# Hybrid attention block: the first eight row blocks of attention groups 1 to 7 are taken in the order 4, 0, 5, 1, 6, 2, 7, 3

## The chip, the cores and the metric

The kernel runs on one core of a Trainium2 chip. The metric is the device time of one execution in microseconds. Before the change it is 2704.64 us, the median of three runs (2703.09 to 2706.77).

The core's engines each work through a list of instructions of their own, in order: TensorE (PE in the profile) multiplies matrices, VectorE (DVE), ScalarE (ACT) and GpSimd (POOL) do the elementwise work, and SyncE (SP) issues DMA transfers. They wait for each other through semaphores.

## What is computed

One layer of a transformer block over 2048 rows of width 1024: normalise, project, two kinds of attention side by side, an output projection, and a gated feed-forward layer (the FFN). Cut to what the change touches:

```python
proj = einsum('bsd,de->bse', rms_norm(h, norm1_w), w_in)
dq, dk, dv, sq, sk, sv = split(proj, SPLIT_POINTS, axis=-1)
# 4 heads of differential attention: two softmax maps per head
p = softmax(dq . dk * scale + bias[t5_bucket(k_pos - q_pos)], masked by chunks of 64)
y_diff = (p[0] - lam * p[1]) @ dv, normalised per head
# 8 heads of stick-breaking attention
z = sq . sk * scale                       # strictly causal: key < query
log_1mb = log_sigmoid(-z)
a = exp(log_sigmoid(z) + reversed exclusive cumsum of log_1mb over the keys)
y_sb = a @ sv, normalised per head
h = h + concat(y_diff, y_sb) @ w_out
h = h + SwiGLU(rms_norm(h, norm2_w))
```

Every query row is independent of every other, so the order in which blocks of rows are taken changes nothing in the result.

## The kernel before

The 2048 rows are 16 row blocks of 128. The attention is done in eight groups, one after the other: groups 0 to 3 are one head of differential attention each (the softmax groups, `diff_attn`), groups 4 to 7 two heads of stick-breaking attention each (`sb_attn`). Both are causal, so row block i needs the keys of blocks 0 to i: its work grows with i, and rows 0 to 3 together have 10 of a group's 136 blocks of scores. ("Row 4" is short for row block 4 below.)

**Projection.** Before a group's attention can read its queries, keys and values, they are projected tile by tile (a tile is one row block; 24 matmuls on line 325, or 72 short ones on line 341 in groups 4 to 6, which are "turned": they come out transposed). In the other groups the tiles are gathered in batches of four: `raw` holds the projected queries and keys, `proj_batch` (lines 386 to 414) squares, sums, takes a root (`rs`, a power on POOL), scales, splits each number into two halves of 16 bits (`st`), and turns the batch with DMA transposes (line 409) into `qT` and `kT`. Group 7 has only the split and the transposes. Batch 1, tiles 4 to 7, has to be there before row 4's scores can be made.

**Softmax row** (`probs`, lines 521 to 569): scores in PSUM (`sc`, line 506); VectorE copies them out with the running maximum (line 542, and line 546 where the bias applies); ScalarE takes the exponential with its sum (line 556); VectorE combines the two maps (lines 561 to 566); `split_t` (lines 449 to 461) splits the result into two halves (`s16`; casts on ScalarE or POOL, the subtraction on POOL, line 98) and turns it with a DMA transpose into `aT`; then the values are multiplied in (`pv`, line 517) two row blocks later.

**Stick-breaking row** (`stage_a`, lines 602 to 627): scores; two sigmoids on ScalarE (lines 618 and 619); a running product over the keys on VectorE (line 621); a product (line 622); `split_t`; and `pv` some seven pieces later (`pend`).

**Accumulators.** The values of four row blocks (two in group 7) share one PSUM accumulator `yp`. After the last of them `finish` (lines 464 to 496) squares, sums, scales, turns on TensorE (line 488), writes two halves `mo` (lines 492 and 493) and stores. There are two `yp` buffers, taken in turn; a buffer is free again when `mo` is written. `aT` has six buffers.

**Order.** The Python loops emit instructions with a priority; a scheduler that runs when the kernel is built then lays out each engine's list. Scores and the row's elementwise work have a higher priority (`"at": 200`), projections a lower one (`"pm": -200`), so projections are put where TensorE would have nothing better. `advance` (line 778) emits the projection tiles, eight ahead at a group's end: when group g starts, tiles 0 to 7 of it have been emitted. The main loop is at lines 862 to 868; the output projection's row blocks are mixed into group 7, then the FFN follows.

Of the kernel before, what the change touches and what calls it, by code (L numbers as in the profile page):

```python
# [11 lines left out]
F32 = mybir.dt.float32  # L12
# [47 lines left out]
def block(tc, a, out):  # L60
# [3 lines left out]
    with top:  # L64
# [44 lines left out]
        def nm(s):  # L109
            uid[0] += 1  # L110
            return f"{s}{uid[0]}"
# [144 lines left out]
        with ExitStack() as ph1:  # L256
# [207 lines left out]
            def finish(g, G, i, k, yp, ssum=None):  # L464
# [30 lines left out]
                note("D", 350 * k + 200)  # L495
                SP.dma_start(ms[i - k + 1 : i + 1, :, g, :].rearrange("i p n -> p i n"), mo[:, :k].rearrange("p i s n -> p i (s n)"))

            def fq(g, i):
                k = 2 if g == NG - 1 else 4
                return (i % k, k)  # L500
# [18 lines left out]
            def diff_attn(g, G):  # L519
                @pri("at")  # L520
                def probs(i):
                    L = (i + 1) * 128
                    near = max(0, i - 1) * 128
                    nb = i // 8 + 1
                    zs = [[], []]
                    if i % 4 == 0:
                        sums[0] = sm.tile([P, 4, 2], F32, tag="sums", bufs=3, name=nm("sums"))
                    su = sums[0][:, i % 4, :]
                    mx = sm.tile([P, 2, 8], F32, tag="mx", name=nm("mx"))
                    for m in range(2):  # L530
                        nx = 0
                        for b in range(nb):
                            n = min(1024, L - 1024 * b)
                            z = z4()
                            for c in range((n + 511) // 512):
                                lo, hi = 512 * c, min(512 * c + 512, n)
                                sc = ps.tile([P, 512], F32, tag="sc", bufs=4, name=nm("sc"))
                                score_chunk(G, sc, i, 2 * b + c, m, (hi - lo) // P)
                                f = min(max(near - 1024 * b - lo, 0), hi - lo)
                                note("D", 1.05 * (hi - lo) + 200)  # L540
                                if f > 0:
                                    DVE.tensor_scalar(z[:, lo : lo + f], sc[:, :f], kz_d[:], None, op0=ALU.mult, op1=ALU.max, accum_out=mx[:, m, nx : nx + 1])
                                    nx += 1
                                if f < hi - lo:
                                    b0 = 1024 * b + lo + f - (i - 1) * 128
                                    DVE.tensor_tensor_reduce(z[:, lo + f : hi], sc[:, f : hi - lo], bias[:, g, b0 : b0 + hi - lo - f], kz_d[:], -3.0e38, ALU.add, ALU.max, mx[:, m, nx : nx + 1])
                                    nx += 1
                            zs[m].append((b, n, z))
                    ng = sm.tile([P, 2], F32, tag="ng", name=nm("ng"))
                    if nx > 1:  # L550
                        DVE.tensor_reduce(ng[:], mx[:, :, :nx], op=ALU.max, axis=AX.X)
                    ACT.activation(ng[:], ng[:] if nx > 1 else mx[:, :, 0], AF.Identity, bias=lnc[:], scale=-1.0)
                    s2 = sm.tile([P, 2, 2], F32, tag="s2", name=nm("s2")) if nb > 1 else None
                    for m in range(2):
                        for b, n, z in zs[m]:
                            ACT.activation(z[:, :n], z[:, :n], AF.Exp, bias=ng[:, m : m + 1], accum_out=(s2[:, m, b : b + 1] if nb > 1 else su[:, m : m + 1]))
                            note("A", 0.84 * n + 300)
                    if nb > 1:
# [3 lines left out]
                    DVE.tensor_scalar(rc[:], rc[:], mlam[:], su[:, 0:1], op0=ALU.mult, op1=ALU.mult)  # L562
                    note("D", 600)
                    aTs = []
                    for (b, n, z0), (_, _, z1) in zip(*zs):
                        DVE.scalar_tensor_tensor(z0[:, :n], z1[:, :n], rc[:], z0[:, :n], op0=ALU.mult, op1=ALU.add)
                        note("D", 1.05 * n + 130)
                        aTs.append((b, n, split_t(z0[:, :n], n)))
                    return aTs

                sums = {}
                ypd = {}

                def values(i, aTs, ssum):
                    r, k = fq(g, i)
                    if r == 0:
                        ypd[0] = ps.tile([P, 512], F32, tag="yp", name=nm("yp"))
                    yp = ypd[0]
                    for q, (b, n, aT) in enumerate(aTs):
                        pv(G, yp, P * r, aT, b, n, 0, 128, r == 0 and q == 0, r == k - 1 and q == len(aTs) - 1)  # L580
                    if r == k - 1:
                        finish(g, G, i, k, yp, ssum)

                held = []
                for i in range(NT):
                    if i % 4 == 0:
                        level()
                    held.append((i, probs(i), sums[0]))
                    if len(held) > 2:
                        values(*held.pop(0))  # L590
                    yield ((i + 1) * (i + 2) / 2 + CD * (i + 1)) / (136 + 16 * CD), i + 1
                for u in held:
                    values(*u)

            def sb_attn(g, G):
# [39 lines left out]
                def stage_c(i, m, b, n, aT):  # L635
                    r, k = fq(g, i)
                    if i // k not in ypd:
                        ypd[i // k] = ps.tile([P, 512], F32, tag="yp", name=nm("yp"))
                    yp = ypd[i // k]
                    pv(G, yp, P * r + 64 * m, aT, b, n, 128 * m, 64, r == 0 and m == 0 and b == i // 8, r == k - 1 and m == 1 and b == 0)  # L640
                    if m == 1 and b == 0 and r == k - 1:
                        finish(g, G, i, k, yp)
                        G["fin"] = i + 1

                pend = []
                done = 0
                for i in range(NT):
                    if i % 4 == 0:
                        level()
                    for b in range(i // 8, -1, -1):  # L650
                        for m in range(2):
# [5 lines left out]
                            yield done / (272 + 48 * CS), (i + 1 if b == 0 and m == 1 else i)  # L657
                for u in pend:
                    stage_b(*u)

# [199 lines left out]
            outs = 0  # L860
            advance(NT - LAG0)
            for g in range(NG):
                advance(NT * g + 4)
                for fr, i in (diff_attn if g < 4 else sb_attn)(g, Gs[g]):
                    advance(max(NT * g + min(4 * (i // 4 + 1), NT), int(NT * (g + 1 + fr) - (LAG * (1 - LF * fr * (g == NG - 1)) if g else LAG0 + (LAG - LAG0) * fr))))
                    while g == NG - 1 and len(wos) == 4 and outs < Gs[g].get("fin", 0) and (outs + 2) * (outs + 3) / 272 < fr - LO:
# [431 lines left out]
```

## Time and profile before

| | |
|---|---|
| median of three runs | 2704.64 us |
| profiled execution: its time | 2702.93 us |
| its span in the profile | 2701.0 us (1.93 us lie around it) |
| first projections and group 0, to its last score | 0 to 203 us |
| groups 1 to 3 (softmax), to the last score of group 3 | 203 to 602 us |
| groups 4 to 6 (stick-breaking), to the last score of group 6 | 602 to 1086 us |
| group 7 with most of the output projection | 1086 to 1351 us |
| the rest of the output projection and the FFN | 1351 to 2701 us |

A group is counted here from the last score of the group before it, since the engines run on across the border. The FFN is nearly all matmuls. The change touches the starts of groups 1 to 7, from the last score of row 15 to the first score of row 8 of the next group: 406.6 us in sum.

How to read the rows: the table of stretches gives, for each stretch, its length, then each engine's busy time and number of instructions, the granted TensorE clock (1.00 is full), the share of the DMA engines' time and the rate. A group of instructions gives line, engine, operation, tiles, shapes and count, then busy time, the mean ns of one, and the idle time before them with what ended it. A row of the timeline gives start and length in us, and in brackets the idle time before it and what ended it. Matmuls overlap, so that the mean of one is longer than the time from one to the next; busy time over count is nearer to that.

### The profile page before, as it was taken

What the parts mean: (1) busy time and instruction counts of PE and PEld (TensorE: products, weight loads), DVE (VectorE), ACT (ScalarE), POOL (GpSimd) and SP (SyncE); (2) the same over time, 40 slices, a digit from 0 to 9 for tenths busy, and PEclk for the clock granted to TensorE, in tenths of its full rate; (3) what the DMA queues carried; (4) which work ended last, traced back from release to release, by engine and by line L of the source; (5) the groups of instructions that cost most, each with busy time, mean ns of one, the idle gap of its engine ahead of it and who ended that gap; (6) DMA issues with size and microseconds to landing.
All of it is one profiled execution on the core that took longest, in us unless ns stands there. A gap on an engine that the chain in (4) does not pass through costs nothing. (4 is left out here: it accounts for less than half of the span.)

```text
span 2701.0 us, 50505 instructions
## 1 busy us (share of the span) xinstructions
PE 2508.6 (93%) x19628; PEld 1507.6 (56%) x19628; DVE 1959.8 (73%) x3712; ACT 1344.7 (50%) x2487; POOL 1517.8 (56%) x1097
## 2 busy tenths in 40 slices
PE   7998989899988989889999999999999999999999
PEld 4655656577776776567774444444444444444444
DVE  6898879899989889887866877778685543433434
ACT  4665656567978878765634534435352112111121
POOL 2578767768767767545665755665564332322323
PEclk9999999999999999999999999999999999999999
DMA  6778697768989989997996566565748744635532
GB/s 221 211 163 184 143 200 172 172 145 183 195 175 185 178 166 206 208 205 203 230 317 232 211 232 219 207 239 183 253 171 330 304 159 157 234 132 184 202 110 94
DMA packets 619584, 534.40 MB, mean 198 GB/s; under 512 B 480640, under 2 KB 548224, under 8 KB 609104
## 3 DMA queue, kind: packets, MB, share of 16 engines
q1 hardware_dynamic: 617520, 529.09, 70.1%
q8 instruction: 154, 2.52, 0.4%
q0 software_dynamic: 512, 1.36, 0.2%
q14 instruction: 86, 0.70, 0.1%
q10 hardware_dynamic: 1312, 0.72, 0.1%
HBM read 261.08 MB, written 147.32 MB: 151 GB/s over the span
## 5 line engine op out<-in xcount | busy, mean ns | idle before, releaser
L98 POOL TENSOR_TENSOR s<-z,s 128x1024 f16<-128x1024 f32 (+7 forms) x288 | 471.5, 1646 | 141.8 <-ACT s L89 118.2
L506 PE MATMUL sc<-kT,qT 128*128 128x512 f16 (+3 forms) x1520 | 382.7, 354 | 51.1 <-DVE z L622 18.6
L1104 PE MATMUL pd<-wd,act 128*128 128x512 f16 x1764 | 392.8, 380 | 5.3 <-DVE cu L1038 4.7
L621 DVE TENSOR_TENSOR_SCAN z<-z,sc 128x512 f32<-128x512 f32 (+3 forms) x320 | 352.8, 1112 | 56.5 <-ACT sc L619 34.6
L325 PE MATMUL pj<-w,xt 128*128 128x384 f16 x1920 | 354.6, 333 | 17.1 <-ACT raw L374 5.8
L1004 PEld LDWEIGHTS <-wu 128*128 128x128 f16 x1848 | 181.9, 98 | 224.6 <-issue 12.8
L1004 PEld LDWEIGHTS <-wg 128*128 128x128 f16 x1848 | 181.3, 98 | 222.9 <-issue 9.3
L517 PE MATMUL yp<-v,aT 128*128 128x64 f16 (+1 forms) x4896 | 271.2, 205 | 36.9 <-DMA aT<-s 35.7
L517 PEld LDWEIGHTS <-aT 128*128 128x128 f16 x4896 | 239.1, 100 | 114.4 <-DMA aT<-s 46.7
L98 POOL TENSOR_TENSOR act<-cg,act 128x512 f16<-128x512 f32 x109 | 150.7, 1393 | 259.4 <-ACT act L1063 259.4
L1104 PEld LDWEIGHTS <-act 128*128 128x128 f16 x1764 | 172.9, 98 | 213.5 <-issue 7.2
L325 PEld LDWEIGHTS <-xt 128*128 128x128 f16 x1920 | 187.8, 99 | 147.2 <-issue 23.4
L89 ACT CAST s<-z 128x128 f16<-128x128 f32 (+7 forms) x215 | 173.3, 810 | 135.9 <-DMA aT<-s 44.6
L98 POOL TENSOR_TENSOR stages<-stages 128x512 f32<-128x512 f32 x97 | 171.4, 1767 | 116.5 <-DVE wg L220 42.2
L618 ACT ACTIVATE z<-sc,c 128x512 f32<-128x512 f32 (+3 forms) x320 | 211.2, 665 | 24.4 <-PE sc L506 12.4
L98 POOL TENSOR_TENSOR hs<-hs,cu 128x512 f32<-128x512 f32 x102 | 133.6, 1317 | 159.3 <-DVE hs L1110 59.7
L506 PEld LDWEIGHTS <-qT 128*128 128x128 f16 x1520 | 128.8, 99 | 119.7 <-issue 23.9
L831 PE MATMUL po<-wo,mt 128*128 128x256 f16 x1536 | 182.4, 279 | 12.6 <-DVE xf L834 8.6
L1063 ACT CAST act<-cg 128x512 f16<-128x512 f32 x126 | 76.7, 616 | 231.1 <-DVE cg L1069 192.7
L1110 DVE SCALAR_TENSOR_TENSOR hs<-pd,c,hs 128x512 f32<-128x512 f32 x144 | 106.0, 747 | 115.0 <-PE pd L1104 105.3
L341 PE MATMUL pj<-xt,w 128*128 128x128 f16 x2304 | 177.4, 222 | 6.2 <-DVE v L363 5.2
L1004 PE MATMUL pm<-X,wu 128*128 128x512 f16 x792 | 179.8, 381 | 2.1 <-ACT cg L1049 1.7
(254 smaller groups left out, 4812.3 us busy)
## 6 DMA issues: line engine op xcount, KB each, us to landing
xt<-xs SPq DMA_DIRECT2D x112, 512.0 KB, 4.5
hs<-hd SPq DMA_DIRECT2D x72, 512.0 KB, 4.5
hd<-hs SPq DMA_DIRECT2D x56, 512.0 KB, 5.9
split<-wg SPq DMA_DIRECT2D x11, 1792.0 KB, 6.9
split<-wu SPq DMA_DIRECT2D x11, 1792.0 KB, 6.7
split<-wd SPq DMA_DIRECT2D x11, 1792.0 KB, 6.8
wg<-split SPq DMA_DIRECT2D x11, 1792.0 KB, 7.5
wd<-split SPq DMA_DIRECT2D x11, 1792.0 KB, 9.0
```

The lines of the kernel that those rows point to most:

```text
L89: ACT.copy(dst, src)
L98: (DVE if e == "D" else POOL).tensor_tensor(dst, a_, b_, op)
L325: PE.matmul(pj[:, :384], lhsT=xv[:, xi, kt, :], rhs=G["w"][:, wi, kt, :], start=n == 0, stop=n == 23)
L341: PE.matmul(o, lhsT=x_ if c == 2 else w_, rhs=w_ if c == 2 else x_, start=n == 0, stop=n == 23)
L506: last = PE.matmul(sc[:, : 128 * w].rearrange("p (t n) -> p t n", n=P), lhsT=G["q"][i // 4][:, a_, i % 4, :], rhs=G["k"][q][:, b_, 0:w, :] ...
L517: PE.matmul(yp[:, y0 : y0 + wd], lhsT=aT[:, a_, :], rhs=v[:, v_ : v_ + wd], start=start and j == 0 and q == 0, stop=stop and j == nb - 1 a ...
L618: ACT.activation(om[:, lo:hi], sc[:, :w], AF.Sigmoid, scale=G["nkz"][:])
L621: DVE.tensor_tensor_scan(ov, ov, sc[:, :w], om[:, hi : hi + 1], op0=ALU.mult, op1=ALU.bypass)
L831: PE.matmul(po[:, sl], lhsT=mt[:, kt, P * xi : P * xi + P], rhs=wos[2 * h + n][wi][:, kt, :], start=q == 0, stop=q == 23)
L1004: PE.matmul(ps_[:].rearrange("p (t n) -> p t n", n=P), lhsT=wv[:, wo, wi, 128 * kt : 128 * kt + 128], rhs=X[xo][:, :, xi, kt, :], start=st ...
L1104: PE.matmul(po[:], lhsT=act[:, ao, xi, 128 * j : 128 * j + 128], rhs=W["d"][:, wo, wi, :], start=start and u == 0 and q == 0, stop=u == nu ...
L1110: DVE.scalar_tensor_tensor(dst, po[:], kd[:], src, op0=ALU.mult, op1=ALU.add)
```

## The change

Groups 1 to 7 take their first eight row blocks in the order 4, 0, 5, 1, 6, 2, 7, 3, and then 8 to 15 as before. Group 0 keeps the old order. What depended on rows coming in turn is now kept by number: the sums and the accumulator belong to i // 4, so two accumulators are open at once; the count of finished rows is kept as a set; the progress that paces the projections is summed over the rows taken; and group g starts only after eight of its tiles have been emitted, not four.

```diff
+            def row_order(g):
+                pairs = [i for j in range(4) for i in (4 + j, j)]
+                return (pairs if g > 0 else list(range(8))) + list(range(8, NT))
...
-                        sums[0] = sm.tile([P, 4, 2], F32, tag="sums", bufs=3, name=nm("sums"))
-                    su = sums[0][:, i % 4, :]
+                        sums[i // 4] = sm.tile([P, 4, 2], F32, tag="sums", bufs=3, name=nm("sums"))
+                    su = sums[i // 4][:, i % 4, :]
...
-                        ypd[0] = ps.tile([P, 512], F32, tag="yp", name=nm("yp"))
-                    yp = ypd[0]
+                        ypd[i // 4] = ps.tile([P, 512], F32, tag="yp", name=nm("yp"))
+                    yp = ypd[i // 4]
...
-                for i in range(NT):
-                    if i % 4 == 0:
+                order = row_order(g)
+                done = 0
+                for at, i in enumerate(order):
+                    if at % 4 == 0:
                         level()
-                    held.append((i, probs(i), sums[0]))
+                    held.append((i, probs(i), sums[i // 4]))
                     if len(held) > 2:
                         values(*held.pop(0))
-                    yield ((i + 1) * (i + 2) / 2 + CD * (i + 1)) / (136 + 16 * CD), i + 1
+                    done += i + 1 + CD
+                    yield done / (136 + 16 * CD), max(order[: at + 2])
...
-                        G["fin"] = i + 1
+                        ended.update(range(i - k + 1, i + 1))
+                        G["fin"] = next(t for t in range(NT + 1) if t not in ended)
...
-                advance(NT * g + 4)
+                advance(NT * g + 4 * (row_order(g)[0] // 4 + 1))
```

What the scheduler makes of it is seen in the engines' lists. First, ScalarE where group 5 starts. L618 and L619 (L625 and L626 in the change) are the two sigmoids, with the width of the chunk at the end; a row of 512 columns with number 11454 is the last of group 4's row 15; L89 is a cast of `split_t`, L349 the copy-out of a projected pair of tiles, L475 and L153 belong to `finish`. Before:

```order
L619 ACTIVATE sc_11454<-sc_11454,c_6511 128x512
L618 ACTIVATE z_11752<-sc_11754,c_8728 128x128
L619 ACTIVATE sc_11754<-sc_11754,c_8727 128x128
L89 COPY s_11414<-z_11395 128x1024
L618 ACTIVATE z_11769<-sc_11771,c_8728 128x128
L619 ACTIVATE sc_11771<-sc_11771,c_8727 128x128
L349 ACTIVATE qT_10979<-pj_10981,half_79 128x256
L618 ACTIVATE z_11786<-sc_11788,c_8728 128x256
```

and with the change:

```order
L626 ACTIVATE sc_11454<-sc_11454,c_6508 128x512
L89 COPY s_11414<-z_11395 128x1024
L349 ACTIVATE qT_10214<-pj_10578,half_79 128x256
L89 COPY s_11462<-z_11443 128x1024
L349 ACTIVATE qT_10979<-pj_10981,half_79 128x256 x2
L475 ACTIVATE y_11735<-yp_10871 128x512
L153 ACTIVATE yrs_11739<-yss_11736,c_6507 128x8
L625 ACTIVATE z_11752<-sc_11763,c_8718 128x512
L626 ACTIVATE sc_11763<-sc_11763,c_8717 128x512
L625 ACTIVATE z_11752<-sc_11754,c_8718 128x128
```

The sigmoids of rows 0 and 1 (128 and 256 wide) stood right behind row 15; now casts, copies and a `finish` stand there, and the next sigmoids are row 4's (512 + 128 wide).

Second, POOL where group 2 starts. `rs839`, `raw808` and `st807` are batch 1 of group 2 (the power, the product with the gain and the two subtractions); L93 and L98 on `s16` are the casts and subtractions of `split_t` for a row, 128 to 384 wide for rows 0 to 2; L219 splits the next group's weights. Before:

```order
L156 TENSOR_TENSOR rs839_4403<-rs839_4403,mh1_77 128x16
L93 TENSOR_SCALAR s16853_4550<-z4847_4532 128x128
L93 TENSOR_SCALAR s16862_4574<-z4856_4556 128x256
L219 TENSOR_SCALAR w16889_4680<-wst888_4676,sW893_4684 128x1536 x2
L93 TENSOR_SCALAR s16871_4601<-z4865_4580 128x384
L98 TENSOR_TENSOR s16853_4550<-z4847_4532,s16853_4550 128x128
L98 TENSOR_TENSOR s16862_4574<-z4856_4556,s16862_4574 128x256
L98 TENSOR_TENSOR raw808_4174<-raw808_4174,gk_222 128x4x128
L98 TENSOR_TENSOR st807_4173<-raw808_4174,st807_4173 128x4x2x64
```

and with the change:

```order
L219 TENSOR_SCALAR w16885_4677<-wst884_4673,sW889_4681 128x1536 x2
L98 TENSOR_TENSOR s16802_4125<-z4788_4077,s16802_4125 128x896
L156 TENSOR_TENSOR rs839_4403<-rs839_4403,mh1_77 128x16
L93 TENSOR_SCALAR s16828_4285<-z4813_4234 128x1024
L98 TENSOR_TENSOR s16830_4291<-z4816_4243,s16830_4291 128x1024
L98 TENSOR_TENSOR s16828_4285<-z4813_4234,s16828_4285 128x1024
L98 TENSOR_TENSOR raw808_4174<-raw808_4174,gk_222 128x4x128
L98 TENSOR_TENSOR st807_4173<-raw808_4174,st807_4173 128x4x2x64 x2
```

Five instructions of rows 0 to 2 and two of the weights stood between the power and the gain of batch 1; now three of group 1's row 15 do, and the weights come earlier.

Third, TensorE in group 2, where `finish` turns the accumulator of rows 4 to 7 and row 8's values are multiplied in. L488 is the turn of `finish` (`yp942` is rows 4 to 7 before, `yp906` rows 0 to 3 with the change, where the turn of rows 4 to 7, `yp878`, stands 17 rows further up); `yp1029` is the accumulator of rows 8 to 11, `aT978` and `aT973` row 8. Before:

```order
L517 LDWEIGHTS aT978_5080
L517 MATMUL yp1029_5325<-v806_4172,aT978_5080 128x128
L488 MATMUL yp942_4885<-id32_63,y1004_5219 128x128 x4
L517 LDWEIGHTS aT978_5080
L517 MATMUL yp1029_5325<-v806_4172,aT978_5080 128x128
```

and with the change:

```order
L488 MATMUL yp906_4730<-id32_63,y1004_5219 128x128 x4
L510 LDWEIGHTS qT1034_5413
L510 MATMUL sc1086_5678<-kT781_4050,qT1034_5413 128x512
L510 LDWEIGHTS qT1034_5413
L510 MATMUL sc1086_5678<-kT781_4050,qT1034_5413 128x512
L510 LDWEIGHTS qT1034_5413
L510 MATMUL sc1087_5682<-kT837_4399,qT1034_5413 128x512
L510 LDWEIGHTS qT1034_5413
L510 MATMUL sc1087_5682<-kT837_4399,qT1034_5413 128x512
L521 LDWEIGHTS aT973_5068
L521 MATMUL yp1029_5325<-v724_3713,aT973_5068 128x128
```

Row 8's values ran while rows 4 to 7 were being finished; now they stand behind the turns of both accumulators.

More of the change, by code (lines that the diff above doesn't have):

```diff
@@ L642, in stage_c @@
                         finish(g, G, i, k, yp)
-                        G["fin"] = i + 1
+                        ended.update(range(i - k + 1, i + 1))
+                        G["fin"] = next(t for t in range(NT + 1) if t not in ended)
                 pend = []
                 done = 0
-                for i in range(NT):
-                    if i % 4 == 0:
+                ended = set()
+                order = row_order(g)
+                for at, i in enumerate(order):
+                    if at % 4 == 0:
                         level()
@@ L656, in sb_attn @@
                             done += n // P + CS
-                            yield done / (272 + 48 * CS), (i + 1 if b == 0 and m == 1 else i)
+                            yield done / (272 + 48 * CS), (max(order[: at + 2]) if b == 0 and m == 1 else max(order[: at + 1]))
                 for u in pend:
```

## The prediction, made before the changed kernel had run

> **What bounds the kernel now.** I read the page's first and fourth parts, then the table of stretches around each group's start, then groups of instructions by line and form, and last the timeline at two places.
>
> ```profile
> PE 2508.6 (93%) x19628; PEld 1507.6 (56%) x19628; DVE 1959.8 (73%) x3712; ACT 1344.7 (50%) x2487; POOL 1517.8 (56%) x1097
> 1443.25 2.76 PE pd L1004 x12
> ```
>
> The second row is where the chain of waits begins: followed back from the end it stays in the FFN and says nothing of the attention. The change touches only the attention, so the question is when that ends, and this has to be read from stretches. First the seven starts, each from the last score of row 15 to the first score of row 4 of the next group, and their sum:
>
> ```profile
> 203.40:223.90 20.50, 17.48 (x173) 12.34 (x171) 19.48 (x62) 15.09 (x39) 17.54 (x10) 0.99 0.65 152
> 336.70:378.70 42.00, 35.83 (x296) 24.59 (x295) 27.03 (x79) 21.59 (x62) 31.45 (x23) 0.92 0.84 171
> 469.30:513.50 44.20, 36.87 (x309) 24.43 (x306) 36.08 (x85) 23.82 (x67) 34.78 (x22) 0.92 0.69 167
> 602.40:624.30 21.90, 19.80 (x291) 18.17 (x289) 19.24 (x47) 17.51 (x36) 15.30 (x12) 0.92 0.82 202
> 760.80:777.80 17.00, 14.83 (x269) 13.05 (x266) 13.86 (x30) 11.19 (x25) 12.29 (x10) 0.90 1.14 219
> 918.20:936.40 18.20, 13.94 (x285) 12.17 (x282) 16.02 (x34) 11.07 (x24) 11.75 (x9) 1.00 0.93 188
> 1086.10:1120.90 34.80, 30.24 (x326) 20.04 (x325) 30.58 (x62) 20.59 (x43) 24.23 (x18) 1.00 0.90 198
> sum 198.60, PE 168.99 PEld 124.79 DVE 162.29 ACT 120.86 POOL 147.33; mean PE 24.14 PEld 17.83 DVE 23.18 ACT 17.27 POOL 21.05
> ```
>
> Then the sum of the seven stretches from row 4's first score to row 8's, with group 1's as one row of them, and the sum of the stretches from there to the group's last score (for group 7, to 1351 us):
>
> ```profile
> 223.90:254.90 31.00, 27.27 (x185) 15.97 (x186) 28.89 (x79) 15.49 (x44) 22.95 (x18) 0.90 0.84 197
> sum 208.00, PE 178.50 PEld 126.89 DVE 175.24 ACT 148.32 POOL 125.26; mean PE 25.50 PEld 18.13 DVE 25.03 ACT 21.19 POOL 17.89
> sum 741.00, PE 681.59 PEld 516.55 DVE 651.77 ACT 536.56 POOL 515.99; mean PE 97.37 PEld 73.79 DVE 93.11 ACT 76.65 POOL 73.71
> ```
>
> TensorE is busy 85% of the starts, 86% of rows 4 to 7 and 92% of the rest; VectorE 82%, 84% and 88%. No engine bounds the first 407 us: TensorE idles 29.6 us in the starts and 29.5 us in rows 4 to 7. This is the most that a better order could take directly from those stretches. After row 8 TensorE is nearer to being the bound than VectorE.
>
> **The change, part by part.** *1. The starts.* Rows 0 to 3 leave the start; row 4 becomes the first row and waits for batch 1. In groups 1 to 3 this batch is late because its chain shares engines with rows 0 to 3. At group 3:
>
> ```profile
> 472.57 1.05 ACT L392 ACTIVATE st<-raw 128x1024 f32<-128x1024 f32 x1
> 480.03 4.03 POOL L219 TENSOR_SCALAR w<-wst,sW 128x1536 f16<-128x1536 f32 x2 [1.19 <-PE pj L325]
> 493.06 2.71 DVE L399 TENSOR_TENSOR raw<-raw,rs 128x1024 f32<-128x1024 f32 x1
> 507.33 1.26 SPq L409 DMA_TRANSPOSE qT<-st  x1
> ```
>
> From the square (472.6) to the transpose (507.3) pass 35 us, of which these steps themselves take few. In the new POOL list batch 1 comes right behind row 15, so the chain gets shorter. How much earlier row 4 can start I take from TensorE's new list: between row 15's last score and row 4's first stand, over the seven starts, 427 projection matmuls of line 325, 258 of line 341 and 795 value matmuls. Their pace is busy time over count:
>
> ```profile
> L325 PE MATMUL pj<-w,xt 128*128 128x384 f16 x1920 | 354.6, 333 | 17.1 <-ACT raw L374 5.8 <-ACT xt L682 4.0 <-DVE st L363 3.5
> L341 PE MATMUL pj<-xt,w 128*128 128x128 f16 x2304 | 177.4, 222 | 6.2 <-DVE v L363 5.2 <-POOL z L622 0.9
> L517 PE MATMUL yp<-v,aT 128*128 128x64 f16 (+1 forms) x4896 | 271.2, 205 | 36.9 <-DMA aT<-s 35.7
> ```
>
> That is 0.185, 0.077 and 0.055 us, so 79 + 20 + 44 = 143 us if nothing waits. With TensorE's present idle share of 15% it would be 168 us. I take half of that share, 155 us: the projections at the start no longer compete with rows 0 to 3 for their copy-out, but batch 1 can still be late, in group 7 above all. Row 4 starts 199 - 155 = 44 us earlier in sum (bounds 31 and 56). Group 4 has most of its own: its list puts 6 matmuls before row 4, against 21.9 us now. In group 5 the wait gets no shorter, and ScalarE and VectorE have little to do in it.
>
> *2. Rows 0 to 3, now among 4 to 7.* The work that lay beside the wait follows it. By the rows
>
> ```profile
> L621 DVE TENSOR_TENSOR_SCAN z<-z,sc 128x512 f32<-128x512 f32 x224 | 284.5, 1273 | 26.6 <-ACT sc L619 18.1 <-ACT z L619 2.1 <-PE yp L517 1.1
> L621 DVE TENSOR_TENSOR_SCAN z<-z,sc 128x128 f32<-128x128 f32 x32 | 14.9, 467 | 11.7 <-ACT sc L619 7.8 <-PE yp L517 2.2 <-ACT z L619 1.2
> L622 DVE TENSOR_TENSOR z<-sc,z 128x512 f32<-128x512 f32 x164 | 111.5, 682 | 3.3
> L546 DVE CUSTOM_DVE_ANT_0 z<-sc,bias,c 128x256 f32<-128x256 f32 x96 | 45.6, 476 | 4.3 <-POOL s L98 4.0 <-PE sc L506 0.3
> L566 DVE SCALAR_TENSOR_TENSOR z<-z,rc,z 128x256 f32<-128x256 f32 x8 | 7.0, 870 | 0.0
> L562 DVE TENSOR_SCALAR rc<-rc,c,sums 128x1 f32<-128x1 f32 x64 | 17.1, 267 | 0.7
> ```
>
> a stick-breaking group has two heads x four running products of 128 to 512 columns, (467 + 1273) / 2 ns on the mean, = 7.0 us, and 2 x 1280 columns of line 622 at 682 / 512 ns = 3.4 us: 10.4 us of VectorE. A softmax group has two maps x 6 copies out of PSUM, all taken at line 546's 476 ns, 4 x 870 and 8 x 267 ns = 11.3 us. Over three and four groups this is 75 us. Rows 4 to 7 then carry 175 + 75 = 250 us of VectorE work where the stretch was 208 us long. At 93%, the share of group 1's stretch above, they last 269 us: 61 us longer (42 us at 100%, 89 us at today's 84%). I take 93% because eight mixed rows overlap better than four. Parts 1 and 2 give 61 - 44 = +17 us at row 8 (bounds -14 and +58).
>
> *3. TensorE is ahead there.* The list puts more projections before row 8's first score than before: 28, 21, 0, 0, 0, 0, 21 matmuls of line 325, 82, -41, 43 and 53 of line 341 (groups 3 to 6), and 27 more of the values. At the paces above: 70 x 0.185 + 137 x 0.077 + 27 x 0.055 = 25 us of work done early. It comes back after row 8 as far as TensorE is the bound there. With TensorE at 92% and VectorE at 88% I take half: -12 us (bounds 0 and -25).
>
> *4. The accumulators.* Both are open in the first eight rows, so row 8's values wait until rows 4 to 7 are finished. At group 1 now (rows 7 and 8, `finish`, row 8's end, and four transposes, two of row 10 and two of row 11):
>
> ```profile
> 279.91 0.55 PE L517 MATMUL yp<-v,aT 128*128 128x128 f16 x7
> 291.06 0.34 PE L517 MATMUL yp<-v,aT 128*128 128x128 f16 x3 [0.37 <-DMA aT<-s]
> 293.98 0.44 PE L517 MATMUL yp<-v,aT 128*128 128x128 f16 x5
> 296.80 0.74 DVE L493 SCALAR_TENSOR_TENSOR mo<-yp,c,mo 128x512 f16<-128x512 f32 x1
> 305.11 8.85 SPq L460 DMA_TRANSPOSE aT<-s  x4
> ```
>
> Row 7's values end at 280.5 and `mo` is written at 297.5: a buffer stays taken for 17 us, and row 8 begins at 291.1. It would begin 6.5 us later. What is queued behind is not TensorE, which has scores and projections, but the transposes: row 11 reuses row 8's `aT`, which row 8's values leave at 294.4, and its transposes come after 305, so over 10 us are to spare. I take 0.5 us a group, +3 us (bounds: 0, and 7 x 6.5 = 45 us if nothing covered it). Which DMAs are issued does not change; in SP's queue a late `aT` would hold up the tile loads behind it, which is in the upper bound. The counters, the sums and `advance` cost nothing: `advance` had eight tiles out at each border anyway.
>
> *Sum.* 17 - 12 + 3 = +8 us on the profiled execution's 2702.9 us. That run lies 1.7 us below the median of 2704.6 us, so against the median the forecast is 2712 us, a little slower. By the bounds alone it could be 2704.6 - 14 - 25 = 2666 us or 2704.6 + 58 + 45 = 2808 us; both need every part at one end.
>
> **The rivals.**
>
> *a. TensorE is the bound and is fed better: faster.* If VectorE runs the mixed rows at 98% (255 us, +47 us), the starts lose 50 us, and three quarters of the early projections come back (-19 us) at no cost of accumulators, the sum is -22 us: 2683 us. For it speak TensorE's 93% of the span and the mixture of long and short rows; against it VectorE's 84%, which shows more waiting for others than lack of work.
>
> *b. The clock recovers: faster.* The granted clock is 0.92, 0.92, 0.92 and 0.90 in four of the starts. Here is the longest wait in them:
>
> ```profile
> 500.85 7.89 PE L325 MATMUL pj<-w,xt 128*128 128x384 f16 x30 [3.43 <-ACT raw L374]
> ```
>
> Were TensorE fed without such gaps, the starts of 42.0, 44.2, 21.9 and 17.0 us would get back 0.08, 0.08, 0.08 and 0.10 of their length, 10.3 us; alone, with parts 1 to 4 cancelling, this gives 2694 us. [...]
>
> *c. The accumulators decide: much slower.* If `aT` had no time to spare, for instance since rows 9 and 10 fill all six buffers while row 8 waits, the stall would reach `split_t`, then VectorE, in each group. Half of the 45 us with +17 and none of part 3 gives 2704.6 + 40 = 2744 us. It decides from the point where row 8 starts over 10 us later than now.
>
> *d. Nothing.* The work is the same and TensorE's list is about full, so what the starts gain is given back by row 8 exactly: 2705 us. That the order is not changed at all is excluded by the lists: row 4's first score precedes row 0's in all seven groups.
>
> **How the numbers follow.** My forecast (slower by a few us) has 0.42, c 0.10, d 0.20, a 0.20, b 0.08. What a measurement of this kernel can tell from no change is about 0.2%, 5.4 us. So slower 0.52, same 0.20, faster 0.28. The forecast's own range is 2706 to 2722 us; with a tenth left out at each side, into a and into c, the range is 2686 to 2729 us.
>
> **What would show it.** Right: the first exponentials or sigmoids of row 4 come 30 to 56 us earlier in sum, and in group 5 no earlier; the stretches from row 4 to row 8 sum to 255 to 290 us with VectorE above 90%; row 8's values start behind `mo` of rows 4 to 7, without idle time of VectorE or ScalarE before row 11's casts; the rest sums to less than 741 us. Wrong: the two first sums together fall below 400 us (then a, or b if the clock stands at 1.00 in the starts), or the rest grows beyond 741 us (then c). The prediction fails if VectorE's share in the mixed rows is not near 93%: each percent is 2.9 us.

## The result, and the profile after

The changed kernel takes 2729.68 us (median of four runs, 2729.06 to 2730.58) against 2705.11 us before (2703.09 to 2706.77): ratio 1.0088, 95% interval 1.0076 to 1.0101. It is 24.6 us slower. The forecast was 8 us, with a range of 2686 to 2729 us; taken from the 2704.64 us that the prediction starts from, the ratio is 2728.4 us, at the very end of that range. The profiled execution took 2729.06 us, with these first lines:

```profile
span 2727.3 us, 50514 instructions
PE 2513.2 (92%) x19628; PEld 1510.9 (55%) x19628; DVE 1947.3 (71%) x3710; ACT 1345.6 (49%) x2492; POOL 1516.2 (56%) x1094
```

Of the 26.3 us between the two spans, 21.8 lie in groups 1 to 7. The table of stretches, one row from the last score of group 0 to that of group 7, before and after (length, then busy time of TensorE, its weight loads, VectorE, ScalarE and POOL, the granted clock, the DMA share and rate):

```profile
203.40:1348.10 1144.70, 1026.17 (x11960) 765.39 (x11958) 986.50 (x2127) 802.85 (x1656) 786.62 (x568) 0.97 0.85 185
```
```profile
202.00:1368.50 1166.50, 1031.25 (x11976) 769.34 (x11974) 977.04 (x2124) 803.96 (x1661) 785.66 (x564) 0.96 0.84 182
```

The same matmuls are there. TensorE idles 135.3 us instead of 118.5, and its work takes 5.1 us longer, at a clock of 0.96 for 0.97. So the loss is mostly TensorE waiting (16.7 us). The other 5.1 us go with the lower clock; that the clock is their whole cause is not shown. (The remaining 4.5 us are -1.4 in group 0 and +5.9 after the last score of group 7, 3.4 of them in the FFN, whose work the change leaves alone.)

Now the three stages of the prediction. After the change, the start of groups 3 to 5 and the sum of the seven starts:

```profile
465.20:500.00 34.80, 28.94 (x244) 19.58 (x243) 23.38 (x46) 14.79 (x30) 29.54 (x15) 0.95 0.97 222
597.40:597.50 0.10, 0.10 (x6) 0.10 (x4) 0.10 (x3) 0.10 (x1) 0.00 (x0) 1.00 0.03 5
757.90:776.70 18.80, 14.48 (x337) 13.85 (x334) 9.15 (x18) 6.16 (x10) 9.31 (x6) 1.00 1.04 201
...
sum 149.70, PE 126.18 PEld 91.91 DVE 102.15 ACT 61.36 POOL 111.12; mean PE 18.03 PEld 13.13 DVE 14.59 ACT 8.77 POOL 15.87
```

Then the mixed rows, from row 4's first score to row 8's, in groups 2 to 6, and their sum over seven groups:

```profile
365.80:394.20 28.40, 27.65 (x192) 16.33 (x193) 22.64 (x90) 19.55 (x54) 11.79 (x13) 1.00 0.70 176
500.00:526.30 26.30, 26.07 (x246) 18.04 (x244) 21.04 (x85) 18.04 (x51) 11.64 (x13) 1.00 0.65 171
597.50:651.20 53.70, 39.14 (x517) 30.91 (x515) 43.85 (x85) 45.74 (x94) 38.23 (x32) 0.93 0.80 159
776.70:824.30 47.60, 40.16 (x531) 33.67 (x531) 39.12 (x84) 35.12 (x71) 27.44 (x25) 0.89 0.73 142
936.80:986.20 49.40, 41.20 (x618) 34.23 (x618) 36.90 (x75) 34.83 (x70) 25.35 (x23) 0.97 0.76 152
...
sum 284.00, PE 240.63 PEld 173.99 DVE 226.52 ACT 205.22 POOL 156.23; mean PE 34.38 PEld 24.86 DVE 32.36 ACT 29.32 POOL 22.32
```

And the rest, to each group's last score, as a sum, before and after (both to row 15's last score of group 7; the prediction's 741.0 us went to 1351 us):

```profile
sum 738.10, PE 678.68 PEld 513.73 DVE 648.98 ACT 533.66 POOL 514.05; mean PE 96.95 PEld 73.39 DVE 92.71 ACT 76.24 POOL 73.44
```
```profile
sum 732.80, PE 664.43 PEld 503.44 DVE 648.37 ACT 537.37 POOL 518.32; mean PE 94.92 PEld 71.92 DVE 92.62 ACT 76.77 POOL 74.05
```

So the starts give 48.9 us (198.6 - 149.7), rows 4 to 7 take 76.0 (284.0 - 208.0) and the rest gives 5.3: +21.8 us. The stages behave differently in the two kinds of groups. In the mixed rows of groups 2 and 3 TensorE is busy 97 and 99%: it is the bound there. In the stick-breaking groups no engine is. In group 4 the same stretch before the change was

```profile
624.40:652.70 28.30, 24.31 (x345) 19.32 (x343) 25.90 (x53) 25.50 (x57) 18.51 (x20) 1.00 0.88 176
```

with VectorE busy 92% of it, for 82% after (43.85 of 53.70 us). Group 6 shows what happens instead; the timeline, TensorE's, ScalarE's and VectorE's rows apart (start, length, and in brackets the idle time before):

```profile
956.02 0.25 PE L521 MATMUL yp<-v,aT 128*128 128x64 f16 x3 [0.92 <-DVE mo L493]
957.72 3.63 PE L341 MATMUL pj<-xt,w 128*128 128x128 f16 x37 [1.45 <-DVE v L363]
961.18 2.06 PE L510 MATMUL sc<-kT,qT 128*128 128x384 f16 x10
```
```profile
962.35 0.69 ACT L625 ACTIVATE z<-sc,c 128x512 f32<-128x512 f32 x1 [5.49 <-PE sc L510]
```
```profile
966.00 3.23 DVE L628 TENSOR_TENSOR_SCAN z<-z,sc 128x384 f32<-128x384 f32 x3 [6.80 <-ACT z L626]
```

TensorE has row 0's first values next and waits for a free accumulator (0.92 us, until `mo` is written), then it waits for VectorE to copy a projected pair out (1.45 us) and works through 37 matmuls of tile 8; only behind them stands row 6's score. ScalarE has waited 5.49 us for it, VectorE 6.80 us for ScalarE. Each engine follows its list, and in turn each waits for the one whose list has something else first. Over the whole run this agrees with what is seen in the page's group of VectorE's running products, before and after:

```profile
L621 DVE TENSOR_TENSOR_SCAN z<-z,sc 128x512 f32<-128x512 f32 (+3 forms) x320 | 352.8, 1112 | 56.5 <-ACT sc L619 34.6
```
```profile
L628 DVE TENSOR_TENSOR_SCAN z<-z,sc 128x512 f32<-128x512 f32 (+3 forms) x320 | 353.1, 1112 | 71.4 <-ACT sc L626 45.6
```

The work is the same to 0.3 us; the waiting before it has grown from 56.5 to 71.4 us.

### The profile page after: what moved, and what is told of

Read it like the earlier page. It is cut to its first block, busy times and chain, and to the rows that moved or that the text cites. A ratio compares the mean times of both kernels' runs of the same rounds, so it can differ in the third digit from the quotient of the medians.

```text
span 2727.3 us, 50514 instructions
## 1 busy us (share of the span) xinstructions
PE 2513.2 (92%) x19628; PEld 1510.9 (55%) x19628; DVE 1947.3 (71%) x3710; ACT 1345.6 (49%) x2492; POOL 1516.2 (56%) x1094
## 5 line engine op out<-in xcount | busy, mean ns | idle before, releaser
L98 POOL TENSOR_TENSOR s<-z,s 128x1024 f16<-128x1024 f32 (+7 forms) x288 | 466.3, 1631 | 132.5 <-ACT s L89 123.5
L510 PE MATMUL sc<-kT,qT 128*128 128x512 f16 (+3 forms) x1520 | 377.1, 351 | 52.6 <-DVE z L628 11.9
L628 DVE TENSOR_TENSOR_SCAN z<-z,sc 128x512 f32<-128x512 f32 (+3 forms) x320 | 353.1, 1112 | 71.4 <-ACT sc L626 45.6
L521 PE MATMUL yp<-v,aT 128*128 128x64 f16 (+1 forms) x4896 | 265.2, 204 | 39.4 <-DMA aT<-s 37.5
L98 POOL TENSOR_TENSOR act<-cg,act 128x512 f16<-128x512 f32 x109 | 151.6, 1400 | 260.5 <-ACT act L1073 260.5
L89 ACT CAST s<-z 128x1024 f16<-128x1024 f32 (+7 forms) x218 | 175.4, 807 | 137.1 <-DVE z L629 28.6
L98 POOL TENSOR_TENSOR stages<-stages 128x512 f32<-128x512 f32 x97 | 169.4, 1747 | 118.7 <-DVE wg L220 42.5
L625 ACT ACTIVATE z<-sc,c 128x512 f32<-128x512 f32 (+3 forms) x320 | 210.3, 663 | 30.0 <-PE sc L510 20.5
L98 POOL TENSOR_TENSOR hs<-hs,cu 128x512 f32<-128x512 f32 x102 | 132.6, 1305 | 165.1 <-DVE hs L1120 62.2
```

Of the source, the lines that this page charges most:

```text
L89: ACT.copy(dst, src)
L98: (DVE if e == "D" else POOL).tensor_tensor(dst, a_, b_, op)
L510: last = PE.matmul(sc[:, : 128 * w].rearrange("p (t n) -> p t n", n=P), lhsT=G["q"][i // 4][:, a_, i % 4, :], rhs=G["k"][q][:, b_, 0:w, :] ...
L521: PE.matmul(yp[:, y0 : y0 + wd], lhsT=aT[:, a_, :], rhs=v[:, v_ : v_ + wd], start=start and j == 0 and q == 0, stop=stop and j == nb - 1 a ...
L625: ACT.activation(om[:, lo:hi], sc[:, :w], AF.Sigmoid, scale=G["nkz"][:])
L628: DVE.tensor_tensor_scan(ov, ov, sc[:, :w], om[:, hi : hi + 1], op0=ALU.mult, op1=ALU.bypass)
```

## The experiments

Diffs are against the changed kernel. Every ratio is against the kernel before, timed on the same chip. The runs are from several chips, on which the kernel before takes 2696 to 2705 us, so go by the ratios and not by the medians. "Group 5" in a table is again the time from the last score of group 4 to the last score of group 5. Each such time is from one profile, and that of the kernel before is from the first chip. Where two kernels have the same TensorE list in a group, its times differ by at most 4.4 us (group 3: 133.1 us before, 128.7 us with rows 1 and 2 of group 4 swapped), so smaller differences of a group say nothing.

**Parts of the change.** The first four runs were to split the loss by groups.

```diff
-                return (pairs if g > 0 else list(range(8))) + list(range(8, NT))
+                return (pairs if 0 < g < 4 else list(range(8))) + list(range(8, NT))
```

> The new order in groups 1 to 3 alone. In the changed kernel these three groups took 3.7 us less than before (133.3, 132.7, 133.1 us before; 131.1, 132.2, 132.1 us after). If groups add up, this is 2701 us (2705 - 4). If the loss of the later groups comes from what the first groups hand on (a clock, a fuller queue), part of the 25 us stays: over 2710 us.

```diff
+                return (pairs if g == 4 else list(range(8))) + list(range(8, NT))
```

> The new order in group 4 alone, where row 4's scores come at once (0.2 us after row 15's). Theory 1 (the loss is the idle vector engines at the start, while row 4 waits for tiles 4 to 7): nothing is waited for here, so no loss, 2702 to 2705 us. Theory 2 (mixing long and short rows itself packs worse in the stick-breaking groups): +2 us as in the changed kernel's group 4, 2707 us.

```diff
+                return (pairs if g > 4 else list(range(8))) + list(range(8, NT))
```

> The new order in groups 5 to 7 alone. Both theories: these three took 23.3 us more (10.2, 4.3 and 8.8), so 2728 us; if the groups interact, 2715 to 2725 us.

```diff
+                return ([4, 5, 6, 7, 0, 1, 2, 3] if g > 4 else list(range(8))) + list(range(8, NT))
```

> Groups 5 to 7 take 4, 5, 6, 7, 0, 1, 2, 3: row 4 still comes first and waits for tiles 4 to 7, but long and short rows are not mixed and the accumulators are filled one after the other. Theory 1 (idle start): nearly the whole loss stays, 2720 to 2728 us. Theory 2 (mixing) and theory 3 (two open accumulators hold row 8 up): at most a third of it stays, 2705 to 2713 us.

| order changed in | median us | ratio, 95% | groups 1 to 4 | 5 | 6 | 7 |
|---|---|---|---|---|---|---|
| nowhere (before) | | 1 | 557.4 | 157.4 | 167.9 | 262.0 |
| groups 1 to 7 (the change) | 2729.68 | 1.0088 (1.0076 to 1.0101) | 555.9 | 167.6 | 172.2 | 270.8 |
| groups 1 to 3 | 2736.13 | 1.0135 (1.0113 to 1.0156) | 559.8 | 171.6 | 176.3 | 263.1 |
| group 4 | 2729.81 | 1.0099 (1.0075 to 1.0122) | 558.1 | 175.1 | 173.4 | 262.5 |
| groups 5 to 7 | 2719.00 | 1.0064 (1.0041 to 1.0088) | 552.1 | 164.2 | 165.6 | 275.7 |
| groups 5 to 7, rows 4 to 7 first | 2723.14 | 1.0084 (1.0064 to 1.0105) | 557.5 | 164.7 | 177.7 | 263.8 |

The parts do not add up: they cost 0.64 to 1.35%, the whole 0.88%. And in the runs with the new order in groups 1 to 3 and in group 4 the loss is not where the order is changed: groups 5 and 6 have the old order there, yet take 23 us more than before. (In the two other runs it lies in groups 5 to 7, which are changed.) Of the expectations, the second case of the first run (over 2710 us) and that of the third (2715 to 2725 us) hold; that of the second fell, with 2730 us for at most 2707. The fourth run keeps nearly the whole loss, 0.84%, though it mixes no rows and fills one accumulator after the other; its expectation reads this for the idle start, but it cannot be told from redrawn lists. The split by groups fell with this. What differs in groups 5 and 6 of the first two is not the order of rows but the lists: the scheduler, having laid out other lists before, puts projections, copies and values elsewhere.

**The layout alone.** So the next runs took the old order in all groups and made a change that should mean nothing: rows 1 and 2, two of the shortest, change places in one group.

```diff
-                return (pairs if g > 0 else list(range(8))) + list(range(8, NT))
+                return [0, 2, 1] + list(range(3, NT)) if g == 1 else list(range(NT))
```

> The old order everywhere, only rows 1 and 2 of group 1 change places. The median of before is taken as 2705 us. Theory A (the layout of before is a lucky one: the time of groups 5 and 6 depends on where the scheduler happens to put projections and their copies, and any change ahead of them loses it): slower by 10 to 25 us, lost in groups 5 and 6. Theory B (the new order leaves projections behind, which groups 5 and 6 then have to make up): within 5 us of before, groups 5 and 6 as before (157 and 168 us).

> The old order everywhere, only rows 1 and 2 of group 4 change places. Theory A: slower by 10 to 25 us, lost in groups 5 and 6, though nothing is moved further than two of the shortest rows. Theory B: within 5 us of before.

With the two rows swapped in group 1: 2735.35 us, ratio 1.0152 (1.0127 to 1.0176). In group 4: 2705.30 us, ratio 1.0034 (1.0021 to 1.0047). Two rows swapped in group 1 cost more than the whole change. Neither theory met both runs: the chip's kernel before takes 2696.09 us, so the swaps cost 39 and 9 us, where theory A had 10 to 25 for each and theory B at most 5. Where the 39 us lie, the table of stretches tells in part; the profiled execution was the slowest of the four (2748.72 us), and of its 41 us over the kernel before in groups 1 to 7, groups 5 and 6 have 24, groups 1 to 4 have 12 and group 7 has 5. Groups 5 and 6, first of the run with the new order in groups 1 to 3, then of the swap in group 1:

```profile
762.60:934.20 171.60, 146.45 (x2210) 119.66 (x2207) 141.89 (x246) 132.15 (x239) 113.87 (x86) 0.93 0.81 168
934.20:1110.50 176.30, 155.16 (x2165) 117.18 (x2162) 149.29 (x271) 132.09 (x243) 116.29 (x89) 0.97 0.88 178
```
```profile
772.60:944.30 171.70, 146.91 (x2209) 119.95 (x2205) 141.90 (x246) 132.22 (x239) 113.83 (x86) 0.93 0.82 168
944.30:1121.60 177.30, 157.47 (x2165) 119.77 (x2162) 149.32 (x271) 132.25 (x243) 116.20 (x89) 0.95 0.87 177
```

They agree to 1 us, and TensorE's list is the same in both from group 5's end to the FFN's end (and, but for four of 732 matmuls, in group 5 up to row 8), instruction by instruction, buffer numbers left out: though one kernel had the new order in groups 1 to 3 and the other only two rows swapped. Groups 5 and 6 of the kernel before and of the swap in group 4, whose TensorE lists are equal there too:

```profile
760.80:918.20 157.40, 142.23 (x2233) 115.05 (x2230) 142.66 (x246) 132.19 (x241) 114.88 (x87) 0.99 0.95 184
918.20:1086.10 167.90, 149.46 (x2088) 113.80 (x2085) 146.98 (x266) 129.78 (x236) 114.06 (x88) 0.97 0.92 186
```
```profile
758.00:914.90 156.90, 140.84 (x2234) 113.75 (x2231) 142.77 (x246) 132.06 (x241) 114.83 (x87) 1.00 0.95 185
914.90:1081.30 166.40, 149.02 (x2088) 113.28 (x2085) 146.87 (x266) 129.80 (x236) 113.92 (x88) 0.97 0.89 187
```

The same rows in the same order take 157 us with one list and 172 us with another. The other engines' work in group 5 is the same to 1 us. What TensorE waited for there, in the swap in group 1 and in the swap in group 4 (us in total, times, longest):

```profile
PE pj L341 <- DVE v L363: 7.4, 3, 4.2
...
PE wsc L182 <- DVE v L363: 4.3, 1, 4.3
```
```profile
PE pj L341 <- DVE v L363: 1.6, 3, 1.2
...
PE wsc L182 <- DVE v L363: 0.3, 1, 0.3
```

With both lists TensorE stands four times before a copy of projections; in the slower one this takes 11.7 us, up to 4.3 at a time, in the other 1.9. The longest in the timeline, TensorE's rows and then VectorE's:

```profile
833.51 0.80 PE L182 MATMUL wsc<-id,m 128*128 128x128 f32 x2 [4.34 <-DVE v L363]
834.23 3.15 PE L509 MATMUL sc<-kT,qT 128*128 128x128 f16 x10
```
```profile
830.88 1.27 DVE L627 TENSOR_TENSOR_SCAN z<-z,sc 128x512 f32<-128x512 f32 x1
832.07 0.46 DVE L350 SCALAR_TENSOR_TENSOR qT<-pj,half,qT 128x256 f16<-128x256 f32 x1
832.44 0.68 DVE L628 TENSOR_TENSOR z<-sc,z 128x512 f32<-128x512 f32 x1
833.04 0.42 DVE L363 SCALAR_TENSOR_TENSOR v<-pj,v 128x256 f16<-128x256 f32 x1
```

The copy (line 363) stands in VectorE's list behind a running product (line 627) and its product (line 628); until 833.5 TensorE cannot go on to the scores at 834.23, since its list has a small matmul for the next weights first (line 182), whose result goes into a PSUM buffer of the kind that this copy empties (tag `pj`). The clock is lower with such waits: 0.93 for 1.00 over the group.

**Twelve tiles ahead.** The same for the pacing of the projections, with the old order as control:

```diff
-LAG0, LAG, PF, CD, CS, LO = 0, 8, 8, 1.0, 1.0, 0.5
+LAG0, LAG, PF, CD, CS, LO = 0, 4, 8, 1.0, 1.0, 0.5
...
+                return (pairs if g > 99 else list(range(8))) + list(range(8, NT))
```

> The old order, but twelve tiles of the next group are emitted at a group's end instead of eight. A control for the next run. Theory A: another layout, so slower by 10 to 25 us like all others. Theory B: the projections are further ahead, so groups 5 and 6 wait no more than before, within 8 us of before.

The new order has the first line of this diff only.

> The changed order with twelve tiles ahead instead of eight. Theory B: the loss of groups 5 and 6 is mostly gone, so at most 10 us above the old order with twelve ahead, and some 2712 us; group 7 keeps its loss of 9 us. Theory A: slower than before by 10 to 25 us, and no nearer to its control than chance makes it.

Old order: 2692.13 us, ratio 0.9980 (0.9964 to 0.9996); it is the only version that came out below both kernels, 0.2% under the one before. New order: 2725.49 us, ratio 1.0107 (1.0090 to 1.0124). Theory B falls: the projections are further ahead and the new order still loses 1.27% to its control. Groups 5 and 6 together are level in these two profiles (351.6 us, and 352.2 in the control), as it said; the new order's loss is in group 7 (252.2 for 235.0 us) and groups 1 to 4 (554.0 for 544.5). But both have 26 to 27 us more in groups 5 and 6 than the kernel before, where theory B expected no more waiting. Theory A as it stood ("all others lose 10 to 25 us") falls too: this layout is no worse than that of before, as it gains at least as much in groups 1 to 4 and 7 as it loses in 5 and 6.

**Order against layout.** What was left to tell is how much the order costs when the layout is drawn anew for both. Two more pairs, with rows 1 and 2 or rows 5 and 6 of group 0 swapped, once under the old order and once under the new:

```diff
+                return ([0, 2, 1, 3, 4, 5, 6, 7] if g == 0 else list(range(8))) + list(range(8, NT))
```

> The old order, only rows 1 and 2 of group 0 change places; TensorE's list differs from that of before in every group. Theory A (layout alone): anywhere from 0 to 1.5% slower than before. Theory C (the order itself costs 0.9%, and the 1.5% of the swap in group 1 was a rare accident): within 0.3% of before.

```diff
+                return ([0, 2, 1, 3, 4, 5, 6, 7] if g == 0 else pairs) + list(range(8, NT))
```

> The changed order in groups 1 to 7, and rows 1 and 2 of group 0 change places. From group 5 on (and in group 3) TensorE's list is that of the changed kernel again, so both theories expect 0.7 to 1.1% slower than before, about the 0.9% of the change. Theory A expects its difference to the run with the old order and the same swap to be within 0.4%, theory C 0.9%.

```diff
+                return ([0, 1, 2, 3, 4, 6, 5, 7] if g == 0 else list(range(8))) + list(range(8, NT))
```

> The old order, only rows 5 and 6 of group 0 change places. In groups 5 and 6 TensorE's list is that of before, so by both theories these take 157 and 168 us as before; theory A leaves up to 0.7% to groups 1 to 4 and 7, theory C expects the time within 0.3% of before.

```diff
+                return ([0, 1, 2, 3, 4, 6, 5, 7] if g == 0 else pairs) + list(range(8, NT))
```

> The changed order in groups 1 to 7, and rows 5 and 6 of group 0 change places. Only group 6 has the list of the changed kernel. Theory A: anywhere from 0.3% to 1.5% slower than before. Theory C: 0.7 to 1.1% slower, and about 0.9% slower than the run with the old order and the same swap.

| otherwise | old order, ratio (95%) | new order, ratio (95%) | difference |
|---|---|---|---|
| as given | 1 | 1.0088 (1.0076 to 1.0101) | 0.88% |
| rows 1, 2 of group 0 swapped | 1.0110 (1.0092 to 1.0128) | 1.0120 (1.0097 to 1.0142) | 0.10% |
| rows 5, 6 of group 0 swapped | 1.0058 (1.0038 to 1.0078) | 1.0103 (1.0087 to 1.0119) | 0.45% |
| twelve tiles ahead | 0.9980 (0.9964 to 0.9996) | 1.0107 (1.0090 to 1.0124) | 1.27% |

Theory C said 0.9% in each of the two new pairs, and they show 0.10 and 0.45%; theory A said at most 0.4% for the first, which holds, but it gives no reason why all four differences should be positive. The new order's 1.20% in that pair lies just above the 0.7 to 1.1% that both theories expected. The changed kernel and the new order with rows 1 and 2 swapped have equal TensorE lists from group 5 on, and agree there to 3 us: 167.6 and 166.9, 172.2 and 175.2, 270.8 and 272.7 us. The old order with rows 5 and 6 swapped has the lists of before in groups 5 and 6 and takes 157.5 and 168.9 us there, for 157.4 and 167.9. The four differences have the mean 0.68% and scatter by 0.51% (standard deviation), so that four of them leave -0.1 to 1.5% (95%, by Student's t) for the order's own cost. The old order's lists spread over 1.7% (0.9980 to 1.0152, six of them), the new order's over 0.3% (1.0088 to 1.0120, four): with eight tiles ahead the five old ones are at 1.0071 on the mean, the three new ones at 1.0104.

## Why the prediction was right, and where it was wrong

The sign was right, the size was not: 24.6 us for a forecast of 8, outside the forecast's own range of 2706 to 2722 us. The sign is in part luck: +8 us is 0.3%, and swapping two short rows under the old order alone moved the time by 0.3 to 1.5%. By its steps:

| | forecast | measured | old order, mean of five lists | new order, mean of three |
|---|---|---|---|---|
| 1. starts and 2. rows 4 to 7, together | 406.6 + 17 | 433.8 | 421.4 (404 to 448) | 438.1 (434 to 442) |
| of it the starts | 155 | 150 | 204.8 | 147.7 |
| of it rows 4 to 7 | 269 | 284 | 216.6 | 290.4 |
| 3. and 4., the rest | 738.1 - 9 | 732.8 | 738.3 | 732.5 |

(The last two columns are the sums of the same stretches, each from one profile, of the runs with eight tiles ahead and the order kept or changed in all of groups 1 to 7, but for a swap of two rows.)

1. *The starts: right.* 149.7 us for 155, so row 4's scores come 48.9 us earlier in sum (forecast 44, bounds 31 and 56). Group 4's wait is gone (0.10 us), and in group 5 it is no shorter (18.8 for 17.0 us), as forecast. Group 3's, where batch 1 was late, went from 44.2 to 34.8 us.

2. *Rows 4 to 7: the step that failed.* "I take 93% because eight mixed rows overlap better than four." VectorE is busy 226.5 of 284.0 us, 80%, less than the 84% before. The sum lies in the forecast 255 to 290 us, but by the prediction's own words it fails if VectorE's share is not near 93%: the mechanism of this step did not hold. Two errors go against each other here. VectorE's work fell by 60.1 us in the starts (162.3 - 102.2) and grew by 51.3 in the mixed rows (226.5 - 175.2), where the prediction moved 75 from the one to the other. And it overlaps worse: the forecast 250 us at 80% would have been 313 us for 269, 44 more; the 23.5 us of work that did not come take 29 off again. This is the 15 us between 269 and 284. The share does not hang on this one layout: with the two swaps of group 0 the new order has 80 and 77% (231.06 of 289.00 and 230.34 of 298.40 us). The five lists of the old order have 77 to 84% in this stretch (176.24 of 227.70 us with rows 1 and 2 of group 1 swapped, 175.24 of 208.00 before), and with twelve tiles ahead it is 90% in the old order and 81% in the new. So no run shows a better overlap of mixed rows. Nor is the bound the one named: in groups 2 and 3 it is TensorE, in groups 4 to 7 none. In group 4 VectorE is busy 44 of 54, ScalarE 46 and TensorE 39 us, each waiting for another's list.

3. *TensorE ahead:* the rest fell by 5.3 us for a forecast of 12, less 3 for part 4; within the bounds. TensorE's busy time in it fell by 14.3 us, and most of that did not shorten it.

4. *The accumulators cost next to nothing.* All waits of TensorE for a written `mo`, in the view of this tile after the change:

```profile
who waited for it (us, times):
  DVE mo L493: 5.3, 4
  PE yp L521: 1.6, 3
```

1.6 us in the whole run, 0.7 before, for a forecast of 3 and bounds of 0 and 45. Row 8's values do start later: from row 8's first score to its first value matmul pass 224 us in sum, 183 before, so some 40 us later, as the upper bound had it (7 x 6.5). But the delay does not reach `split_t`: its casts on ScalarE wait less for a free `aT` than before. Groups 1 to 7, before and after (us in total, times, longest):

```profile
ACT s L89 <- DMA aT<-s: 36.7, 21, 3.7
```
```profile
ACT s L89 <- DMA aT<-s: 15.7, 13, 3.0
```

And the rest fell, where rival c has it grow: c is out for the sum. In group 2 alone row 8's values start 16 us later and the rest takes 71.0 us for 67.3; whether the one is the cause of the other is open.

5. *The other rivals.* Rival a assumed VectorE at 98% in the mixed rows, where it is busy 80%; rival b assumed a clock that recovers where TensorE does not wait, and no run filled the gaps to show that. In the trace of before the clock stood at 0.50 for one stretch in each of its four starts (from 342.8, 499.8, 605.7 and 772.9 us, for 6.8, 6.8, 3.4 and 3.4 us), begun in a wait of TensorE of 3.32 or 3.43 us or up to 0.6 us behind one of 2.10 or 2.15 us. After the change, the clock did rise in group 5's start (0.90 to 1.00), but it stands at 0.93 and 0.89 in the mixed rows of groups 4 and 5, and over groups 1 to 7 it went from 0.97 to 0.96, the other way. Rival d had rows 4 to 7 take exactly what the starts gain; they took 76.0 us for 48.9.

The greater error lies outside these steps. The prediction set each term against one layout of the old order and took it for the old order's time. That layout is a good one: of the five with eight tiles ahead it is the fastest, 19 us (0.71%) below their mean. The forecast for the first two stages, +17 us, is what the means of the last two columns differ by (16.7 us), and with the rest (-5.8 us) they give +11 us where the forecast was +8. This agreement should not be read as a proof, as the old lists alone spread over 44 us there. What is shown: with the old order, lists redrawn by a swap of two short rows or of rows 5 and 6 of group 0 cost 0.3 to 1.5%, and with twelve tiles ahead -0.2%, so the 0.88% cannot be put down to the order alone. What stays open is the share: by the four pairs the order costs 0.68% on the mean, with an interval that touches zero. Which detail of the scheduler's choices sends groups 5 and 6 into the slower list was not tried.

## What to carry to other kernels

Where a scheduler lays out the engines' lists, a change of order redraws every list behind it, also where the code is untouched: compare the stages that should not have changed first, and if they moved, run a few neutral variants of both versions before putting a per cent down to an idea. Kernels whose TensorE lists agree in a group took the same time there to 4.4 us or better, which makes the lists themselves a control. And work moved beside other work should be priced at the busy share that the stage has now, with a better overlap as the hopeful end of the range: here the stage had 84%, and the mixed rows overlapped at 80%, not at 93%.

## What the runs showed of the hardware

The TensorE clock fell without a long wait. Group 5 of the changed kernel in stretches of 3.4 us:

```profile
787.00:790.40 3.40, 3.06 (x43) 2.50 (x40) 2.50 (x7) 3.40 (x10) 2.39 (x4) 1.00 0.88 180
790.40:793.80 3.40, 0.99 (x19) 0.84 (x19) 3.40 (x7) 2.52 (x6) 2.15 (x2) 0.94 0.63 98
793.80:797.20 3.40, 3.37 (x35) 3.37 (x36) 3.30 (x9) 1.95 (x4) 1.92 (x3) 0.55 0.90 270
...
814.20:817.60 3.40, 1.49 (x25) 1.02 (x25) 3.40 (x5) 3.40 (x7) 1.73 (x3) 0.96 0.98 203
817.60:821.00 3.40, 1.94 (x14) 1.67 (x15) 3.40 (x9) 2.61 (x5) 3.32 (x2) 0.50 0.16 32
821.00:824.40 3.40, 3.40 (x37) 3.40 (x36) 3.37 (x16) 0.23 (x1) 2.85 (x3) 0.54 1.68 185
```

TensorE's busy time is the first number after the length, the clock the third from the end. The clock is near half (0.55, then 0.50 and 0.54) for one or two such stretches behind one in which TensorE was busy 0.99 or 1.49 of 3.4 us, and back at 1.00 in the stretches from 797.20 and 824.40. In stretches of 0.1 us it stands at 0.50 from 793.4 to 796.8 us and from 817.3 to 824.1 us, 10.2 us together. The longest single wait of TensorE there was

```profile
793.83 4.26 PE L341 MATMUL pj<-xt,w 128*128 128x128 f16 x48 [1.87 <-DVE v L363]
```

1.87 us. TensorE waited 0.91 us up to 790.97 and was 1.5 us into the next wait when the clock fell at 793.4, and 1.10 us up to 814.83 and 1.0 us into the next when it fell at 817.3. At 0.50 the 43 matmuls of line 341 from 819.86 us took 4.42 us to the next instruction's start, 0.103 us each; at 1.00 the 13 from 785.92 us took 0.72 us, 0.055 each. So by estimate 10.2 us at half the clock cost at most 5.1 us, less where TensorE waits anyway. They make the clock of 0.89 in group 5's mixed rows: 1 - 0.5 x 10.2 / 47.6 = 0.89.
